# A row gradient streamed through three slots: the difference in three VectorE pieces with the halving on ScalarE, instead of one fused VectorE pass

## Chip, cores, metric

The kernel runs on one core of one Trainium2 chip. The metric is the device time of one execution in microseconds (us), as a median of several executions. The profile is one execution taken by the hardware profiler.

## The reference

```python
x = np.random.randn(8192, 8192).astype(np.float32)
return np.gradient(x, axis=1)
```

Inside a row the result is (x[j+1] - x[j-1]) / 2; the two ends take the plain difference of neighbours. The input is 268.44 MB and so is the output.

## The kernel before

A tile is R = 2 rows on each of 128 partitions, 64 KiB per partition; there are 32 tiles and three slots. A tile is loaded 64 elements into its slot, and the result is written from the slot's beginning, partly over the input. The store goes out from there; the next load into the slot waits until that store has landed. Loads are issued by SP (SyncE), stores by ACT (ScalarE), the last two tiles' stores by SP.

```python
    slots = [pool.tile([P, SH + W], f32, name=f"slot{k}", tag=f"slot{k}") for k in range(NB)]   # NB = 3
    ...
    def load(i):
        b = slots[i % NB]
        ins = nc.sync.dma_start(out=b[:, SH : SH + W], in_=x_sets[i])
        loads.append(chain(i, ins, *(stores[i - NB] if i >= NB else [])))
    ...
            ins = nc.gpsimd.tensor_sub(                      # the end differences, on Pool
                out=ends[:, i, :, :],
                in0=xin[:, :, 1 : m : m - 2],
                in1=xin[:, :, 0 : m - 1 : m - 2],
            )
            ...
                ins = nc.vector._custom_dve(                 # (in0 - in1) * 0.5 in one pass
                    dve_ops.TENSOR_TENSOR_REDUCE_SUB_MAX,
                    out=b[:, c0:c1],
                    in0=b[:, SH + c0 + 1 : SH + c1 + 1],
                    in1=b[:, SH + c0 - 1 : SH + c1 - 1],
                    s0=0.0,
                    s1=0.5,
                )
                ...
                ins = placer.tensor_copy(out=res[:, :, 0 : m : m - 1], in_=ends[:, i, r : r + nr, :])
                ...
                cuts = [c0, c0 + FIRST, c1] if i == 1 else [c0, c1]   # store 1 in two pieces
                for a0, a1 in zip(cuts, cuts[1:]):
                    ins = queue.dma_start(out=out_sets[i, :, a0:a1], in_=b[:, a0:a1])
```

The last tile is worked in two halves, so that its first half can be stored early.

## Time and profile before

| | |
|---|---|
| time, first comparison | 1248.27 us median of 4 runs (1247.95 to 1248.54) |
| the run that was profiled | 1252.67 us, 4 us more than any of these |
| DVE (VectorE) busy | 554.8 us, 44% |
| Pool (GpSimd) busy | 8.8 us, 1% |
| both DMA queues' packets | 99.3% of 16 engines' span |
| landing of a tile to its store's issue | 17.7 us (22.74 to 40.44 for the first tile) |

A slot is in one of three states: loading, computing, storing. So the page's last part, the issues of transfers with the median time from issue to landing, gives two of these three. These two lines of the kernel before are what the argument turns on (the last number is the time in us):

```profile
slot<-in_x_dram SPq DMA_DIRECT2D x32, 43.7
out_dram<-slot ACTq DMA_DIRECT2D x29, 55.0
```

An 8.39 MB tile alone at 434 GB/s, the rate of many of the page's slices, would take 19.3 us (an estimate from these two numbers). That a load takes 43.7 and a store 55.0 means that they share the engines (the two queues' packets take 52.9 and 46.4% of the same 16 engines' span) and queue behind one another.

### The profile page before, as it was taken

The numbers are of one execution on the slowest core, as the hardware profiler recorded it, in microseconds if no ns is written. First come the engines' busy times: TensorE is split into PE (matmuls) and PEld (weight loads), VectorE is DVE, ScalarE is ACT, GpSimd is POOL, SyncE is SP. The second block draws the span as 40 slices with busy tenths as digits, with TensorE's granted clock in tenths as the row PEclk, the third lists the DMA queues.
The fourth block names the chain that finished last, engine by engine and source line by source line (L and its number), as shares of the span: only waits on it lengthen the run. The fifth ranks groups of instructions, "written<-read, shape, count | busy, mean of one in ns | idle before, by whom it ended". The sixth has DMA issues, their size and how long they took to land.

```text
span 1250.2 us, 266 instructions
## 1 busy us (share of the span) xinstructions
DVE 554.8 (44%) x54; POOL 8.8 (1%) x48
## 2 busy tenths in 40 slices
DVE  2841455335553255523555335553345533455443
POOL 0000000000000000000000000000000000000000
DMA  9999999999999999999999999999999999999996
GB/s 403 436 438 433 434 434 436 428 436 421 428 434 434 436 430 434 434 436 436 436 436 436 434 436 434 428 432 426 434 434 434 436 434 436 436 436 436 436 436 289
DMA packets 9504, 536.88 MB, mean 429 GB/s; under 512 B 1056, under 2 KB 1056, under 8 KB 1184
## 3 DMA queue, kind: packets, MB, share of 16 engines
q1 hardware_dynamic: 5040, 285.21, 52.9%
q10 hardware_dynamic: 4464, 251.66, 46.4%
HBM read 268.44 MB, written 268.44 MB: 429 GB/s over the span
## 4 chain that ended last, share of the span: by engine, by line
another core or an unknown queue 83%; DMA 9%; issue 3%; DVE 3%; SPq 1%; POOL 0%; POOLq 0%
DMA slot<-in_x_dram 5%; DMA out_dram<-slot 3%; DVE slot L81 3%; SPq L60 1%; DVE slot L92 0%; POOL ends L70 0%; POOLq L131 0%
## 5 line engine op out<-in xcount | busy, mean ns | idle before, releaser
L81 DVE CUSTOM_DVE_ANT_0 slot<-slot 128x16382 f32<-128x16382 f32 (+1 forms) x33 | 551.3, 16706 | 673.0 <-POOL ends L70 673.0
L70 POOL TENSOR_TENSOR ends<-slot 128x4 f32<-128x4 f32 x32 | 6.3, 198 | 993.9 <-DMA slot<-in_x_dram 993.9
L92 DVE COPY slot<-ends 128x4 f32<-128x4 f32 (+1 forms) x21 | 3.6, 171 | 0.7
L92 POOL COPY slot<-ends 128x4 f32<-128x4 f32 x12 | 2.3, 190 | 207.9 <-DVE slot L81 207.9
L120 POOL MEMSET const-bfloat16-1.0<- 128x1 bf16 x1 | 0.1, 102 | 0.0
L120 POOL MEMSET const-uint8-127<- 128x1 uint8 x1 | 0.1, 102 | 0.0
L120 POOL MEMSET const-float32-0.0<- 128x1 f32 x1 | 0.1, 98 | 0.2 <-issue 0.2
L120 POOL MEMSET const-float32-1.0<- 128x1 f32 x1 | 0.1, 98 | 0.0
## 6 DMA issues: line engine op xcount, KB each, us to landing
out_dram<-slot SPq DMA_DIRECT2D x2, 4096.0 KB, 20.3
out_dram<-slot ACTq DMA_DIRECT2D x1, 7744.0 KB, 58.0
slot<-in_x_dram SPq DMA_DIRECT2D x32, 43.7
out_dram<-slot ACTq DMA_DIRECT2D x29, 55.0
out_dram<-slot ACTq DMA_DIRECT2D x1, 448.0 KB, 22.8
out_dram<-slot SPq DMA_DIRECT2D x1, 37.7
```

What stands on the lines that cost most here:

```text
L60: ins = nc.sync.dma_start(out=b[:, SH : SH + W], in_=x_sets[i])
L70: ins = nc.gpsimd.tensor_sub(out=ends[:, i, :, :], in0=xin[:, :, 1 : m : m - 2], in1=xin[:, :, 0 : m - 1 : m - 2],)
L81: ins = nc.vector._custom_dve(dve_ops.TENSOR_TENSOR_REDUCE_SUB_MAX, out=b[:, c0:c1], in0=b[:, SH + c0 + 1 : SH + c1 + 1], in1=b[:, SH + c0 ...
L92: ins = placer.tensor_copy(out=res[:, :, 0 : m : m - 1], in_=ends[:, i, r : r + nr, :])
L120: nc = _bacc.Bacc("TRN2", target_bir_lowering=False, num_devices=1)
```

## The change

Its intent is to do without the custom instruction and without Pool: plain subtracts on DVE in three pieces, each halved on ACT while DVE works on the next. The end copies move to ACT. The small first piece of store 1 goes. The last tile keeps the custom pass.

```diff
-            ins = nc.gpsimd.tensor_sub(
+            ins = nc.vector.tensor_sub(
                 out=ends[:, i, :, :],
...
+                if last:
+                    ins = nc.vector._custom_dve(   # as before
...
+                else:
+                    cuts = [c0, W // 3, 2 * W // 3, c1]
+                    for a0, a1 in zip(cuts, cuts[1:]):
+                        ins = nc.vector.tensor_sub(
+                            out=b[:, a0:a1],
+                            in0=b[:, SH + a0 + 1 : SH + a1 + 1],
+                            in1=b[:, SH + a0 - 1 : SH + a1 - 1],
+                        )
+                        diff = chain(i, ins, *at)
+                        ins = nc.scalar.mul(out=b[:, a0:a1], in_=b[:, a0:a1], mul=0.5)
+                        halved = chain(i, ins, diff)
...
-                placer = nc.gpsimd if i % 5 in (1, 3) and not last else nc.vector
-                ins = placer.tensor_copy(out=res[:, :, 0 : m : m - 1], in_=ends[:, i, r : r + nr, :])
+                ins = nc.scalar.copy(out=res[:, :, 0 : m : m - 1], in_=ends[:, i, r : r + nr, :])
...
-                cuts = [c0, c0 + FIRST, c1] if i == 1 else [c0, c1]
-                for a0, a1 in zip(cuts, cuts[1:]):
-                    ins = queue.dma_start(out=out_sets[i, :, a0:a1], in_=b[:, a0:a1])
-                    stores[i].append(chain(i, ins, placed))
+                ins = queue.dma_start(
+                    out=out_sets[i, :, r * m : (r + nr) * m], in_=b[:, r * m : (r + nr) * m]
+                )
+                stores[i].append(chain(i, ins, placed))
```

More of the change, by code (lines that the diff above doesn't have):

```diff
@@ L31 @@
     W = R * m
-    FIRST = 896
     nsets = n // (P * R)
@@ L79 @@
                 c0, c1 = r * m + 1, (r + nr) * m - 1
-                ins = nc.vector._custom_dve(
-                    dve_ops.TENSOR_TENSOR_REDUCE_SUB_MAX,
-                    out=b[:, c0:c1],
-                    in0=b[:, SH + c0 + 1 : SH + c1 + 1],
-                    in1=b[:, SH + c0 - 1 : SH + c1 - 1],
-                    s0=0.0,
-                    s1=0.5,
-                )
-                halved = chain(i, ins, *at)
+                if last:
+                    ins = nc.vector._custom_dve(
+                        dve_ops.TENSOR_TENSOR_REDUCE_SUB_MAX,
+                        out=b[:, c0:c1],
+                        in0=b[:, SH + c0 + 1 : SH + c1 + 1],
+                        in1=b[:, SH + c0 - 1 : SH + c1 - 1],
+                        s0=0.0,
+                        s1=0.5,
+                    )
+                    halved = chain(i, ins, *at)
+                else:
[9 more added lines that the diff above has]
+                        halved = chain(i, ins, diff)
@@ L90 @@
                 res = b[:, r * m : (r + nr) * m].rearrange("p (t m) -> p t m", m=m)
-                placer = nc.gpsimd if i % 5 in (1, 3) and not last else nc.vector
-                ins = placer.tensor_copy(out=res[:, :, 0 : m : m - 1], in_=ends[:, i, r : r + nr, :])
+                ins = nc.scalar.copy(out=res[:, :, 0 : m : m - 1], in_=ends[:, i, r : r + nr, :])
                 placed = chain(i, ins, halved)
                 queue = nc.scalar if i < nsets - 2 else nc.sync
-                c0, c1 = r * m, (r + nr) * m
@@ L99 @@
-                cuts = [c0, c0 + FIRST, c1] if i == 1 else [c0, c1]
-                for a0, a1 in zip(cuts, cuts[1:]):
-                    ins = queue.dma_start(out=out_sets[i, :, a0:a1], in_=b[:, a0:a1])
-                    stores[i].append(chain(i, ins, placed))
+                ins = queue.dma_start(
+                    out=out_sets[i, :, r * m : (r + nr) * m], in_=b[:, r * m : (r + nr) * m]
+                )
+                stores[i].append(chain(i, ins, placed))
                 at = [halved]
```

## The prediction

> **What bounds the kernel now.** I read the page's first three parts first, because they say at once whether an engine or the transfers carry the span.
>
> ```profile
> span 1250.2 us, 266 instructions
> DVE 554.8 (44%) x54; POOL 8.8 (1%) x48
> DMA  9999999999999999999999999999999999999996
> GB/s 403 436 438 433 434 434 436 428 436 421 428 434 434 436 430 434 434 436 436 436 436 436 434 436 434 428 432 426 434 434 434 436 434 436 436 436 436 436 436 289
> q1 hardware_dynamic: 5040, 285.21, 52.9%
> q10 hardware_dynamic: 4464, 251.66, 46.4%
> ```
>
> The busiest compute engine works 44% of the span; the DMA row is full in 39 of 40 slices and the two queues' packets together take 99.3% of sixteen engines' time. The bytes are fixed: 268.44 MB in, 268.44 MB out. The trace's packet records agree: nearly every 64 KiB packet takes 2.418 us, on either queue. There are 8,192 such rows' worth in all, 512 per DMA engine, so 512 x 2.418 = 1238.0 us that no order of instructions can remove. The first packet begins at 1.8 us. In the landing records of the very last store, most engines finish at 1240.5 to 1242.6 us and the slowest at 1249.3. So the span is the floor, a start of 2 us, and about 9 us by which one DMA engine is late.
>
> Next, is a transfer ever waiting for compute? The groups by shape give the durations, the waits of the sync engine's queue say what releases loads, and the timeline gives one period.
>
> ```profile
> L81 DVE CUSTOM_DVE_ANT_0 slot<-slot 128x16382 f32<-128x16382 f32 x31 | 533.9, 17224 | 654.4 <-POOL ends L70 654.4
> L81 DVE CUSTOM_DVE_ANT_0 slot<-slot 128x8190 f32<-128x8190 f32 x2 | 17.4, 8686 | 18.6 <-POOL ends L70 18.6
> L92 DVE COPY slot<-ends 128x4 f32<-128x4 f32 x19 | 3.3, 172 | 0.6
> L92 POOL COPY slot<-ends 128x4 f32<-128x4 f32 x12 | 2.3, 190 | 207.9 <-DVE slot L81 207.9
> ...
> SPq L60 <- DMA out_dram<-slot: 1156.3, 29, 79.5
> ```
>
> A load into a slot waits for the store out of it, 29 times for 1156.3 us: the queue of loads is held by transfers, not by arithmetic. The chain of waits that ended last shows the same at the tail:
>
> ```profile
> 1174.77 35.83 issue
> 1210.60 0.24 POOLq L131
> 1210.84 0.02 issue
> 1210.87 8.70 DVE slot L81
> 1219.57 0.02 issue
> 1219.59 0.17 DVE slot L92
> 1219.76 8.60 DVE slot L81
> ```
>
> The last load has landed by 1210.6; DVE then needs two passes of 8.7 us, and still 20 us of stores follow. By the landing records the store of the tile before lands on its slowest engine at 1229.9, so both halves of the last tile (issued at 1219.8 and 1228.6) are queued before that engine runs dry.
>
> **A period and its slack.** Loads are issued every 38.7 us (16 packets per engine at 2.418 us are 38.7, so the slowest engine is never idle). A slot goes round in three periods, 116.1 us: median 43.7 us from a load's issue to landing, 17.7 us of compute (the first tile: Pool starts at 22.74, the store goes out at 40.44), 55.0 us from store issue to landing; the sum is 116.4. For both queues to hold at least one transfer all the time, load and store together need two periods, 77.4 us. So compute could take about 38.7 us, twice what it takes, before even one queue ran empty; and a single queue can use all the engines alone: in the first 25 us, with loads alone, the rate is already 419 GB/s.
>
> [...] The custom pass shows just this: (17224 - 8686)/(16382 - 8190) = 1.042 ns per element and 151 ns fixed. [...]
>
> **The change part by part.**
>
> 1. *Difference on DVE.* Pieces of 5460, 5461 and 5461 elements. [...] 5461 x 1.042 + 151 = 5.84 us each, 17.53 us for three, 0.30 more than one pass, for two more fixed costs. The end differences move from Pool (198 ns) to DVE (about 170, as its copies of four elements). DVE in total: 31 x 17.70 + 17.4 + 0.2 = about 566 us, 45%.
>
> 2. *Halving on ACT.* [...]
>
> 3. *End copies on ACT*, after the halving: about 0.19 us, like the 170 to 190 ns of DVE and Pool.
>
> From landing to store issue: [...] 22.7 us, against 17.7: 5.0 us more per tile, 155 us over 31 tiles if all were exposed. By the slack above (about 21 us per slot) none is. What must give is time spent queueing: three periods still make 116.1, so load plus store to landing fall from 98.7 to about 93.5, and since a store is queued behind the one before it, I expect the median store to land about 5 us sooner after issue (near 50 us) with the load's near 43.7. The store's wait shortens, its end doesn't move.
>
> 4. *Head.* The first store moves from 40.4 to about 45.4. The three loads issued at the start are 3 x 19.4 = 58 us of work at full rate, so the engines have work; the load that shared with store 0 now runs alone for those 5 us. Cost 0.
>
> 5. *Tail.* The last tile keeps the custom pass, so 1210.6 to the two stores gains only ACT's hand-off, some 0.1 us each. Store 30 goes out near 1197 instead of 1192.3. The last load lands on its earliest engines at 1201.5, on its slowest at 1210.6, and store 30 is behind it in the same queue: still on time, with 4 us to spare on the earliest engines and 13 on the slowest. Cost 0 to 1.
>
> 6. *Store 1 in one piece.* The small first piece (448 KB, 3.5 KB packets) disappears. Same bytes; eight fewer small packets an engine. What it can move is the phase between the queues, and with it which engine gets late. I put this at a few us of either sign.
>
> Sum: 1248.1 + 0 (steady) + 0 (head) + 0.5 (tail) + about 1 (a tuned phase is disturbed, more likely to lose than to gain) = 1249.5 us.
>
> **The rivals.**
>
> *The latency is exposed.* If slots went strictly one after the other, 31 x 5.0 = 155 us: about 1403. It would need a queue that waits for compute. Against it: the DMA row of nines, and twice the compute time fits. Half-exposed, at head and tail only: 10 us, 1258. Against it: points 4 and 5.
>
> *ACT becomes the bound, or its work delays the stores it issues.* ACT issues stores in its own order, after the copy. [...] If halving were twice as slow [...], the time from landing to store would be about [...] 35 us: nearly at the 38.7 us limit, yet still about 1250. [...]
>
> *The passes contend with the transfers for the buffer memory.* ACT would add a read and a write of every element. For the present passes the windows of the trace show no steady sign:
>
> ```profile
> 515.20:532.40 17.20, 17.18 (x1) 0.00 (x0) 1.00 1.04 450
> 532.40:554.30 21.90, 0.05 (x1) 0.19 (x1) 1.00 1.02 443
> 554.60:571.80 17.20, 17.19 (x1) 0.00 (x0) 1.00 0.98 427
> 571.80:593.30 21.50, 0.17 (x1) 0.00 (x0) 1.00 1.02 439
> ```
>
> With DVE busy 450 and 427 GB/s, with it idle 443 and 439. Bins of whole packets explain such scatter. If ACT slowed transfers by 1%, 1261.
>
> *The lateness of one DMA engine changes.* It is 9 us now, built up by load packets of 2.5 to 3.6 us instead of 2.418, nearly all in the first 660 us. With another phase it could vanish (1241) or double (1258). This is the rival I take most seriously, and it sets the range.
>
> **Range and chances.** Executions of one kernel differ by 0.6 us, so the width is from the phase and a little contention: 1245 to 1256 for 8 in 10. Two per cent is 25 us: 1223 is below the floor of 1238, so faster is all but impossible (0.01). Slower than 1273 needs exposed latency or contention: 0.03.
>
> **What would show each step.** Right: the DMA row stays at 9 in 39 slices and about 434 GB/s; DVE near 45% with 5.8 us pieces; [...] first store near 45.4; store to landing near 50 us at the median; sync's waits for stores still over 1100 us; two or more transfers pending throughout. Wrong: DMA slices below 9 in the middle, or a store-bound wait replaced by one for ACT (latency exposed); packets longer than 2.418 us while ACT runs (contention); full DMA on most engines but a last landing far behind the others (engine lateness).

The 22.7 us from landing to store was a sum with a term for ACT's last piece, which no trace stood behind, and the second rival's 35 us the same. So 22.7 and 35 us stand as estimates. That a plain subtract runs at the custom pass's rate was assumed too. Measured after the prediction: 4755 ns for an ACT piece, 5848 ns for a DVE piece, with the custom pass as with the plain subtract. The forecast's zeros for the middle and the head rest on the 22.7. Its floor of 1238 us rests on the packets: of the 64 KiB ones none is shorter than 2.418 us in the profiles of the two kernels, and 98% (before) and 96% (changed) took under 2.43.

## The result

The changed kernel takes 1249.45 us, median of 4 runs (1248.41 to 1249.82), against 1248.27 us. The ratio is 1.0008, 95% interval 0.9991 to 1.0026: the same. Ratios in this document are the mean time of one kernel's fast runs over that of the other's of the same rounds, so not quite the ratio of the quoted medians.

The head of the changed kernel's page, its two DMA queues and its issues:

```profile
span 1247.6 us, 419 instructions
DVE 566.6 (45%) x127; ACT 450.0 (36%) x127; POOL 0.2 (0%) x4
DMA  9999999999999999999999999999999999999998
q1 hardware_dynamic: 5040, 285.21, 53.1%
q10 hardware_dynamic: 4320, 251.66, 46.6%
...
slot<-in_x_dram SPq DMA_DIRECT2D x32, 43.7
out_dram<-slot ACTq DMA_DIRECT2D x30, 49.6
```

ACT works for 450 us that did not exist before, and the DMA row is as full as it was. The load's median is still 43.7 us; the store's has fallen from 55.0 to 49.6. The work itself, by groups of one shape (busy us and mean ns after the bar):

```profile
L93 DVE TENSOR_TENSOR slot<-slot 128x5461 f32<-128x5461 f32 x62 | 362.6, 5848 | 2.1
L99 ACT ACTIVATE slot<-slot 128x5461 f32<-128x5461 f32 x62 | 294.8, 4755 | 69.9 <-DVE slot L93 69.9
...
L102 ACT COPY slot<-ends 128x4 f32<-128x4 f32 x31 | 6.1, 198 | 1.0
L69 DVE TENSOR_TENSOR ends<-slot 128x4 f32<-128x4 f32 x32 | 5.3, 166 | 655.9 <-DMA slot<-in_x_dram 655.9
```

An ACT piece is shorter than a DVE piece, so ACT waits for each (69.9 us over 62 pieces) and only the third one trails. The timeline of tile 30 shows the order (start, duration, what):

```profile
1171.93 0.17 DVE L69 TENSOR_TENSOR ends<-slot 128x4 f32<-128x4 f32 x1 [20.82 <-DMA slot<-in_x_dram]
1172.13 17.61 DVE L93 TENSOR_TENSOR slot<-slot 128x5460 f32<-128x5460 f32 x3
1178.01 4.75 ACT L99 ACTIVATE slot<-slot 128x5460 f32<-128x5460 f32 x1 [21.89 <-DVE slot L93]
1183.89 4.75 ACT L99 ACTIVATE slot<-slot 128x5461 f32<-128x5461 f32 x1 [1.13 <-DVE slot L93]
1189.77 4.75 ACT L99 ACTIVATE slot<-slot 128x5461 f32<-128x5461 f32 x1 [1.13 <-DVE slot L93]
1194.56 0.20 ACT L102 COPY slot<-ends 128x4 f32<-128x4 f32 x1
1194.78 31.53 SPq L105 DMA_DIRECT2D out_dram<-slot  x3
```

From 1171.93 to 1194.78 are 22.85 us from landing to store; before they were 17.7. The loads still wait for stores and for nothing else:

```profile
SPq L59 <- DMA out_dram<-slot: 1153.8, 29, 79.6
```

Before, 29 such waits made 1156.3 us. A slot's round is 43.7 + 17.7 + 55.0 = 116.4 us before and 43.7 + 22.9 + 49.6 = 116.2 after: the 5.2 us that the tile computes longer came off the time until its store has landed.

The landing records say where. Each transfer lands sixteen times (1056 landings for the 66 transfers of the kernel before), once on each DMA engine, and the page counts to the last. These are medians in us from issue to landing (the last two rows are experiments below, the last of them a slow run):

| run | landing to store | load: first, last engine | store: first, eighth, last engine |
|---|---|---|---|
| before | 17.7 | 40.3, 43.7 | 42.3, 42.6, 55.0 |
| changed | 22.9 | 40.5, 43.7 | 42.7, 43.7, 49.6 |
| after_uncut | 31.6 | 39.5, 43.8 | 39.5, 39.8, 41.6 |
| after_pieces_two_passes | 34.7 | 39.4, 42.5 | 39.1, 40.5, 43.3 |

So on the first eight engines to land, a store took no less time than before. What shrank is the lag of the last engine behind the first, from 12.7 to 7.0 us; the next load into the slot waits for that last one. The three experiments that change one part agree: 42.1 and 49.0 us to the first and the last landing in after_split_store, 43.5 and 55.0 in before_whole_store, 41.1 and 55.2 in after_no_act_halving.

### The profile page after: what moved, and what is told of

Read it like the earlier page. It is cut to its first block, busy times and chain, and to the rows that moved or that the text cites. A ratio compares the mean times of both kernels' runs of the same rounds, so it can differ in the third digit from the quotient of the medians.

```text
span 1247.6 us, 419 instructions
## 1 busy us (share of the span) xinstructions
DVE 566.6 (45%) x127; ACT 450.0 (36%) x127; POOL 0.2 (0%) x4
## 4 chain that ended last, share of the span: by engine, by line
DMA 68%; DVE 14%; another core or an unknown queue 12%; ACT 4%; issue 0%; SPq 0%
DMA out_dram<-slot 35%; DMA slot<-in_x_dram 33%; DVE slot L93 13%; ACT slot L99 3%; DVE slot L81 1%; ACT slot L102 0%; DVE ends L69 0%; SPq L59 0%
## 5 line engine op out<-in xcount | busy, mean ns | idle before, releaser
L99 ACT ACTIVATE slot<-slot 128x5461 f32<-128x5461 f32 (+1 forms) x93 | 442.2, 4755 | 743.4 <-DVE slot L93 743.4
L93 DVE TENSOR_TENSOR slot<-slot 128x5461 f32<-128x5461 f32 (+1 forms) x93 | 543.9, 5848 | 3.2
L69 DVE TENSOR_TENSOR ends<-slot 128x4 f32<-128x4 f32 x32 | 5.3, 166 | 655.9 <-DMA slot<-in_x_dram 655.9
L102 ACT COPY slot<-ends 128x4 f32<-128x4 f32 (+1 forms) x33 | 6.5, 197 | 31.8 <-DVE slot L81 30.8
L81 DVE CUSTOM_DVE_ANT_0 slot<-slot 128x8190 f32<-128x8190 f32 x2 | 17.4, 8691 | 0.1
L99 ACT ACT_TABLE_LOAD x1 | 1.3, 1283 | 0.7 <-PEq L126 0.7
## 6 DMA issues: line engine op xcount, KB each, us to landing
slot<-in_x_dram SPq DMA_DIRECT2D x32, 43.7
out_dram<-slot ACTq DMA_DIRECT2D x30, 49.6
```

The costliest lines, as they stand in the source:

```text
L69: ins = nc.vector.tensor_sub(out=ends[:, i, :, :], in0=xin[:, :, 1 : m : m - 2], in1=xin[:, :, 0 : m - 1 : m - 2],)
L81: ins = nc.vector._custom_dve(dve_ops.TENSOR_TENSOR_REDUCE_SUB_MAX, out=b[:, c0:c1], in0=b[:, SH + c0 + 1 : SH + c1 + 1], in1=b[:, SH + c0 ...
L93: ins = nc.vector.tensor_sub(out=b[:, a0:a1], in0=b[:, SH + a0 + 1 : SH + a1 + 1], in1=b[:, SH + a0 - 1 : SH + a1 - 1],)
L99: ins = nc.scalar.mul(out=b[:, a0:a1], in_=b[:, a0:a1], mul=0.5)
L102: ins = nc.scalar.copy(out=res[:, :, 0 : m : m - 1], in_=ends[:, i, r : r + nr, :])
```

## The experiments

The theory: the DMA engines are the bound, the added 5 us per tile lie in the transfers' waiting time, and ACT's arithmetic does not slow the transfers. The rivals: part of the time shows; ACT's extra traffic slows transfers; or one of the small parts (the split store, Pool) mattered and cancelled something else.

Three figures of each profile's packet records help to read the runs. *Excess*: the packets' time beyond 2.418 us per 64 KiB, summed and divided by the 16 DMA engines. *Idle*: the time to the last packet's end less the packets' time, again per engine. *Drained*: how many transfers were issued onto a queue whose former transfer had landed on all 16 engines (or did so within 1 us). Every kernel moves 1238.0 us of nominal packets per engine. Packet records can overlap a little (two idle times below, 0.0 and 0.4 us, are less than the 1.76 us before the first packet of the kernel before), so an idle time near zero is rough. The rows of after_pieces_two_passes and before_two_slots are profiles of runs that count as slow (1309.94 and 1341.74 us).

| run | slots x tile | landing to store, us | median us | excess, us | idle, us | drained |
|---|---|---|---|---|---|---|
| before | 3 x 64 KiB | 17.7 | 1248.3 | 3.2 | 7.8 | 1 of 66 |
| changed | 3 x 64 | 22.9 | 1249.5 | 4.5 | 4.0 | 1 of 65 |
| after_split_store | 3 x 64 | 22.9 | 1251.5 | 3.1 | 4.5 | 1 of 66 |
| before_whole_store | 3 x 64 | 17.7 | 1256.9 | 2.9 | 8.8 | 1 of 65 |
| after_no_act_halving | 3 x 64 | 18.1 | 1254.3 | 3.4 | 13.3 | 1 of 65 |
| after_uncut | 3 x 64 | 31.6 | 1257.2 | 11.4 | 2.4 | 1 of 65 |
| after_pieces_two_passes | 3 x 64 | 34.7 | 1308.4 | 48.5 | 20.2 | 19 of 65 |
| after_two_act_passes | 3 x 64 | 45.5 | 1354.6 | 58.0 | 57.1 | 46 of 65 |
| after_62us | 3 x 64 | 62.7 | 1393.4 | 55.0 | 96.9 | 59 of 65 |
| before_two_slots | 2 x 64 | 17.7 | 1329.2 | 50.6 | 49.3 | 49 of 66 |
| after_two_slots | 2 x 64 | 22.9 | 1357.2 | 52.8 | 77.0 | 56 of 65 |
| before_half_tiles | 6 x 32 | 9.2 | 1246.9 | 5.7 | 0.0 | 0 of 128 |
| half_tiles_two_passes | 6 x 32 | 23.3 | 1247.3 | 5.5 | 0.4 | 1 of 128 |
| after_half_tiles_uncut | 6 x 32 | 16.2 | 1263.3 | 11.2 | 6.9 | 0 of 128 |

The experiments were noisier than the first comparison: the kernel before itself gave 1246.8 to 1270.6 us (11 runs, median 1252.1) in the first batch, 1246.6 to 1260.1 in the second, 1247.9 to 1258.7 in the third. So medians of different batches must not be compared to a few us; the ratios below are each against the kernel before on the same chip. A run over 1.5% above its kernel's fastest counts as slow and is left out of the ratios.

### Undoing one part, or doing one alone

**after_split_store**: the changed kernel with store 1 in two pieces again.

```diff
-                ins = queue.dma_start(
-                    out=out_sets[i, :, r * m : (r + nr) * m], in_=b[:, r * m : (r + nr) * m]
-                )
-                stores[i].append(chain(i, ins, placed))
+                d0, d1 = r * m, (r + nr) * m
+                for a0, a1 in ([(d0, d0 + 896), (d0 + 896, d1)] if i == 1 else [(d0, d1)]):
+                    ins = queue.dma_start(out=out_sets[i, :, a0:a1], in_=b[:, a0:a1])
+                    stores[i].append(chain(i, ins, placed))
```

> The changed kernel with one part undone: store 1 again in two pieces (448 KB first). Theory (the bytes bind; the split only shifts the phase between the two queues): 1247 to 1251 us, within 0.3% of the changed kernel, ACT and DVE busy times unchanged. Rival (the split was what kept the late DMA engine's lag down): nearer to the kernel before, about 1248.2, and the spread of the last store's sixteen landings different from the changed kernel's 5 us.

Measured: 1251.51 us (1247.87 to 1257.07), ratio 0.9997 (0.9959 to 1.0035), the same. The median is just above the stated range, on a chip where before stood at 1252.05. The landings of the very last store spread over 5.4 us, near the changed kernel's 5.2 (before: 8.8; one profile each). In these profiles the split did not set this spread.

**before_whole_store**: the kernel before with `cuts = [c0, c1]` for every store.

> The kernel before with one part of the change done alone: all stores in one piece, custom pass and Pool work kept. Theory: 1247 to 1251 us, ratio to before within 0.2%. Rival (the split matters): slower than before by over 0.3%, that is over 1252.

Measured: 1256.86 us (1247.84 to 1268.4), ratio 1.0028 (0.998 to 1.0077). The median lies above the range and beyond the rival's 1252, but the interval holds 1, so a cost of the whole store of up to 0.8% is neither shown nor excluded. The last landings spread over 8.9 us, as before's 8.8.

**after_no_act_halving**: the three pieces stay, but each is the custom pass that halves as it subtracts; ACT only places the ends.

```diff
-                        ins = nc.vector.tensor_sub(
+                        ins = nc.vector._custom_dve(
+                            dve_ops.TENSOR_TENSOR_REDUCE_SUB_MAX,
                             out=b[:, a0:a1],
...
+                            s0=0.0,
+                            s1=0.5,
                         )
-                        diff = chain(i, ins, *at)
-                        ins = nc.scalar.mul(out=b[:, a0:a1], in_=b[:, a0:a1], mul=0.5)
-                        halved = chain(i, ins, diff)
+                        halved = chain(i, ins, *at)
```

> The changed kernel with the halving folded back into the custom DVE pass, still three pieces a tile, end copies still on ACT, so ACT does no arithmetic on the bulk. From landing to store about 17.9 us instead of 22.9. Theory (5 us per tile are hidden, ACT does not disturb the transfers): 1248 to 1250.5 us, the same as the changed kernel within 0.2%, but the median store takes about 55 us from issue to landing again instead of 49.6. Rival (ACT's extra reads and writes of the buffer slow transfers, or part of the latency shows): faster than the changed kernel by 0.3% or more, 1245 or less.

Measured: 1254.34 us (1245.81 to 1258.1), ratio 1.0005 (0.9963 to 1.0048); above the range, and so was before on this chip. Taking 442 us of ACT arithmetic away made nothing faster that could be seen; the interval leaves room for 0.4%. As the intervals of these three runs all lie within 0.8% of the kernel before, a larger cost of one of these parts that another cancels is excluded. Pool's work was not undone alone. The groups by shape and the issues of this run:

```profile
L93 DVE CUSTOM_DVE_ANT_0 slot<-slot 128x5461 f32<-128x5461 f32 x62 | 362.6, 5848 | 2.1
...
out_dram<-slot ACTq DMA_DIRECT2D x30, 55.2
```

The custom pass takes 5848 ns, to the nanosecond what the plain subtract takes: halving was free in it. And the store takes 55.2 us again. The round is 44.1 + 18.1 + 55.2 = 117.4: the time from landing to store and the store's time to its last landing trade nearly one for one.

### More latency on the same three slots

**after_uncut**: one subtract, then one ACT pass over the whole tile (`cuts = [c0, c1]`).

> The changed kernel with the tile in one piece: one 17.2 us subtract, then one ACT pass of about 13.9 us, so about 31.6 us from landing to store, 9 us more than with pieces. Theory (compute is hidden as long as it takes under 38.7 us a tile): 1248 to 1252 us; the median store lands about 41 us after its issue instead of 49.6. Rival (latency shows in part): more than the changed kernel by several us, up to 31 x 8.7 = 270 us if all shows. The pieces would be worth nothing if the theory holds.

Measured: 1257.23 us (1253.5 to 1262.16), ratio 1.0045 (1.0004 to 1.0085). ACT's pass took 13.86 us a tile and the subtract 17.22. The store's median fell to 41.6 us as expected, and yet the runs are 0.45% slower than before, some 5.6 us:

```profile
slot<-in_x_dram SPq DMA_DIRECT2D x32, 43.8
out_dram<-slot ACTq DMA_DIRECT2D x30, 41.6
```

That is 2% of the 270 us which full exposure would cost, but it may not be nothing: the interval just leaves out 1. The table says in what form it comes: excess 11.4 us instead of 3.2, that is slower packets, with no more idle time. So the pieces may be worth a little.

The landing records fit a reason. 53 of 63 transfers were issued when the one before them on their queue had landed on some engines already, or did so within 1 us (1 in the changed kernel), and 220 of the 221 store packets that ran 3% or more over 2.418 us start within 4.5 us of a store's issue. But this count alone does not set the loss: it is 31 in after_no_act_halving, whose excess is 3.4 us.

**after_two_act_passes**: uncut, with two ACT passes, so that the result stays right.

```diff
-                        ins = nc.scalar.mul(out=b[:, a0:a1], in_=b[:, a0:a1], mul=0.5)
-                        halved = chain(i, ins, diff)
+                        for by in (2.0, 0.25):
+                            ins = nc.scalar.mul(out=b[:, a0:a1], in_=b[:, a0:a1], mul=by)
+                            halved = chain(i, ins, diff)
```

> Uncut tile and two ACT passes over it (times 2, times a quarter; the result is still right): about 17.4 + 2 x 13.9 + 0.3 = 45 us from landing to store, past the 38.7 us; ACT busy 28 us per period, so no engine binds. Theory (work of the DMA engines never stops while a transfer is queued): past 38.7 us two slots are in compute at once, and at the turn from store to load of the third no transfer is queued for some 1.5 to 2.3 us (0.3 to the landing, 1.1 from issue to the first packet, up to 0.8 of slow first packet): 31 x that on 1249 = 1295 to 1320 us. Rival A (exposure in proportion to the excess): 45 - 38.7 = 6.3 us x 31 = 195: about 1445. Rival B (never exposed before two slots' compute exceeds the period): 1250 to 1255.

Measured: 1354.57 us (1348.38 to 1355.98), ratio 1.0787 (1.0713 to 1.086). All three figures miss: it is less than in proportion and more than one dry turn a tile. The parts of the 1.5 to 2.3 us compare with the first load of the kernel before: its last landing came 0.35 us after its last packet's end, its first packet began 1.02 us after its issue, and each engine's first packet ran 0.08 to 0.99 us over 2.418. The rows of the page for DMA:

```profile
DMA  9799999999999999999999999998999999999999
GB/s 410 333 393 437 434 407 368 370 362 418 372 374 434 434 403 391 408 408 372 403 432 401 401 376 405 403 418 356 403 403 403 403 377 397 352 408 379 377 434 403
```

The reader should note how little the digits show: 9 means 90% or more, and the loss is in GB/s. By the records, 46 of 65 transfers went onto a drained queue, loads and stores alike, where I had counted one turn per tile. The loss beyond the nominal packets is half slow packets (58.0 us) and half idle (57.1). Beyond before's 11.0 us that is 104 us, or 2.3 us for each of the 46. If the whole loss is put on these, the cost of one turn was guessed about right (1.5 to 2.3 us); their number was not.

**after_62us**: the same, with the subtract done twice.

```diff
-                        ins = nc.vector.tensor_sub(
+                        for _ in range(2):
+                            ins = nc.vector.tensor_sub(
...
```

> As the last, and the subtract done twice over on DVE (same values): about 62 us from landing to store, DVE 34.6 and ACT 27.9 us per period of 38.7, so no engine binds yet. Theory: a turn from store to load without any other transfer, once a tile, as at 45 us: 1295 to 1330 us, and the DMA row below full throughout. Rival A (proportional): (62 - 38.7) x 31 = 722 more: about 1970. Rival B: 1250 to 1260.

Measured: 1393.42 us (1391.17 to 1395.71), ratio 1.1113. The result is wrong, against what I wrote: the first subtract overwrites input that the second reads, as the result lies over the input. The two subtracts took 34.48 us and the two ACT passes 27.74 in the tiles whose timeline was read; in after_two_act_passes, whose result is right, one subtract took 17.22 and the two ACT passes 27.74. So the wrong values show in no duration, and the time stands as a measurement of latency only. 59 transfers met a drained queue, and the loss beyond before's is 141 us, 2.4 us each on the same terms. No run came near the proportional 1970 us.

**after_pieces_two_passes**: the changed kernel with those two passes over each of the three pieces: the case that the prediction named.

> The changed kernel, three pieces, with two ACT passes over each (the case that the prediction named: 35 us from landing to store). A round of three periods leaves about 81 us for load and store, against 77.4 for two queues that never run empty. Theory, as mended after the runs at 45 and 62 us (each transfer issued onto an empty queue costs about 2.1 us, one half of it slow packets, one half idle): few such issues, under 15, so 1252 to 1275 us. The prediction said about 1250. Rival A (all time beyond 22.7 us shows in proportion): 31 x 12 = 370 us more. Rival C (more ACT arithmetic itself slows the transfers, as 1354 us with two passes could also be read): near 1354, as there are the same two passes.

Measured: 1308.38 us: three runs of 1306.8 to 1310.9 and one of 1286.08. The three count as slow only because the one is 1.5% quicker, so no ratio is given; every run is over 2% above the slowest run of before in its batch (1258.73). So at 34.7 us from landing to store, which leaves more than two periods for load and store, the time rises already, and neither the prediction's "still about 1250" nor my mended 1252 to 1275 held. Rivals A (370 us more) and C (near 1354) missed too. The issues of its profile, a slow run:

```profile
slot<-in_x_dram SPq DMA_DIRECT2D x32, 42.5
out_dram<-slot ACTq DMA_DIRECT2D x30, 43.3
```

Both are over the 38.7 us of a period, yet 19 transfers met a drained queue. The loss beyond before's is 58 us there, 3.0 us for each of the 19, so drained queues are hardly all of it.

### Is it ACT's work, or the latency?

**half_tiles_two_passes**: the very kernel that took 1354.6 us, with tiles of one row per partition and six slots. Bytes in flight and arithmetic per byte are the same; only the time from landing to store, and the size of one step and of its packets, halve.

```diff
-    R = 2
-    NB = 3
+    R = 1
+    NB = 6
```

> The uncut tile with two ACT passes that took 1354 us, now with tiles of half the size and six slots: the same bytes in flight, the same arithmetic per byte, about 23 us from landing to store against a period of 19.4 and a round of 116. Theory (what costs is an empty queue, and here 93 us are left for load and store where 38.7 keep both queues filled): 1246 to 1257 us, at most three issues onto an empty queue. Rival C (two ACT passes slow the transfers): over 1330 again.

Measured: 1247.28 us (1247.1 to 1247.33), ratio 0.9962 (0.9929 to 0.9995).

```profile
DVE 566.5 (45%) x128; ACT 899.2 (72%) x191; POOL 0.2 (0%) x4
...
GB/s 404 421 438 438 422 437 438 432 427 438 437 426 434 437 437 423 437 437 431 429 438 437 426 432 438 437 424 436 438 429 429 438 438 424 435 438 435 425 437 391
...
slot<-in_x_dram SPq DMA_DIRECT2D x64, 4096.0 KB, 43.6
out_dram<-slot ACTq DMA_DIRECT2D x62, 4096.0 KB, 49.3
```

ACT is busy for 899 us, twice as long as in the changed kernel, and the transfers run at full rate. This shows that the 1354.6 us did not come from ACT's traffic by itself but from latency against three coarse slots. The round is six periods: 43.6 + 23.3 + 49.3 = 116.2 us.

**before_half_tiles**: the kernel before with R = 1, NB = 6 and whole stores.

> The kernel before with tiles of half the size, six slots and all stores whole. Theory: the two queues were never empty before, so there is nothing to win in the middle: 1244 to 1253 us, within 0.4% of before. Rival (packets of 32 KB cost more): over 1260.

Measured: 1246.94 us (1246.82 to 1247.56), ratio 0.996 (0.9933 to 0.9987), with 71.3 + 9.2 + 35.6 = 116.1 us a round. It is 0.4% better than the kernel before, and steady: its runs lie within 0.8 us on a chip where before's lie within 11 (those of half_tiles_two_passes within 0.3). The landings of its last store spread over 1.5 us: the engines finish nearly together.

**after_half_tiles_uncut**: the changed kernel uncut, with R = 1, NB = 6.

> The changed kernel uncut, with tiles of half the size and six slots: about 16.5 us from landing to store. Theory: the 0.45% that the uncut tile cost with three slots goes away, 1244 to 1253 us, the same as before within 0.3%, and the DMA engines' excess over 2.418 us per 64 KiB falls from 11 us to 3 to 5. Rival (the cut itself, ACT working beside DVE, was what helped): 1253 to 1260 again.

Measured: 1263.28 us (1254.97 to 1276.53), ratio 1.0067 (1.0022 to 1.0113). This misses. Two ACT passes took 1247.3 us, one takes longer. No queue drained, but the excess is 11.2 us, with 611 packets that ran over their 1.213 us by more than 0.05 us (47 and 42 in the two other half-tile runs), and the landings of its last six stores spread over 10 to 25 us. So slow packets come also where neither latency nor an empty queue explains them. That takes weight from after_uncut too: its excess of 11.4 us may have the same unknown cause, and not its thin margin. What makes a given order of the two queues fall into or out of this, no run here settles.

### Two slots

**before_two_slots** and **after_two_slots**: NB = 2 in either kernel.

> The kernel before with two slots instead of three. From landing to store 17.7 us, and a slot's round is two periods. Theory: while one slot computes only the other transfers, and its turn from store to load falls in the middle of that time, so 1.5 to 2.3 us per tile are lost: 1295 to 1320 us. Rival (buffer count sets how much of the compute shows): 31 x some 10 us more, over 1500.

> The changed kernel with two slots. Theory: the loss is the turn alone, not the compute time, as long as that is under 38.7 us: the same as the kernel before with two slots within 0.5%, 1295 to 1320 us. Rival (with scarce slots the 5 us more show): 31 x 2.5 to 5 us more than the kernel before with two slots, 80 to 155 us.

Measured: before 1329.23 us over all runs (1299.49, 1316.73, and two called slow, 1341.74 and 1346.15), ratio of the fast ones 1.0433 (1.0315 to 1.055); changed 1357.15 us (1355.04 to 1371.19), ratio 1.0847 (1.0767 to 1.0927). The changed kernel is slower than before here: the theory's "the same within 0.5%" fails, the rival's 80 to 155 us too. 49 transfers in the one and 56 in the other met a drained queue. The size of the difference is uncertain, since before with two slots varies by 47 us; its direction is not, as every run of the one is above every run of the other. So with three slots the change is free and with two it costs some 4%. That it is the 5 us of latency, and no other part of the change, that costs there is argued: with two slots no part was undone alone.

## Why the prediction was right, point by point

- **The bound.** Right. The DMA row stayed full; ACT gained 450 us of work and the time moved by 1.2 us, within noise.
- **DVE.** 17.53 us for three pieces was worked out, 17.61 measured (the timeline), 566.6 us busy against "about 566". The fixed part was read as 151 ns; the two lengths leave 150 (17224 - 1.0422 x 16382). Nothing hangs on it.
- **ACT.** 4.755 us a piece and 450.0 us busy, 36%, were measured. The profile also has an ACT_TABLE_LOAD of 1283 ns, at 0.73 us into the span and out of the way: the first tile's load landed at 22.6.
- **Landing to store.** 22.7 put down, with an estimate in it for ACT's piece; 22.85 measured.
- **Where it is hidden.** The median store was to land near 50 us after issue and the load to stay near 43.7; they are 49.6 and 43.7. after_no_act_halving gives the 55 us back. This is the step that carries the prediction, and as a sum it is shown by measurement. Its reason, that the store is queued behind the one before it, is only half right: to the first engine's landing the store took 42.3 us before and 42.7 after. What gave way was the last engine's lag.
- **Head.** The first store was to move to about 45.4; it went out at 45.50.
- **Tail.** Store 30 went out at 1194.78, not 1197, because the whole schedule of that profile is 2.6 us earlier; the last load landed at 1208.1, after it, as needed.
- **Store 1 and the phase.** "A few us of either sign" is as much as can be said after the runs too. The 1.2 us between the medians is not resolved.
- **The sum.** 1248.1 + 0.5 + 1 is 1249.6, not 1249.5. That 1249.45 was measured is luck at this closeness: the 1.5 us were guesses for the tail and the phase, and in the experiments one kernel's runs differ by some 10 us.
- **What was wrong in it.** The second rival's aside: at about 35 us from landing to store the time would be "still about 1250". Measured: 1286 to 1311. The step that failed is the slack: it was taken as sharp at 38.7 us, and counted on the median of the last engine's landing. A large cost is there at 34.7 us, and a first, small one (0.45%) perhaps at 31.6. A load is issued only when the last engine's part of a store has landed (0.02 to 0.09 us after it in the kernel before), and until then the engines that landed first get nothing new for that slot: for 12.7 us at the store's median. In the kernel before the first engine had 40.3 + 42.3 = 82.6 us of load and store, 5 us over two periods and not 21; the other 16 us were waiting for the last engine. In these profiles the added latency came out of that lag first, without a visible cost. In after_uncut 4.3 us of lag were left at the load and 2.1 at the store, which puts the limit at 38.7 - 6.4 = 32.3 us: an estimate made after the runs, which no run of its own tested. Also "executions differ by 0.6 us" held in the first comparison alone.
- **The lateness of one engine.** The rival taken most seriously. In the profiles the spread of the last landings goes with the latency (8.8 and 8.9 us at 17.7, 8.9 at 18.1, 5.2 and 5.4 at 22.9, 2.3 at 31.6), one profile each, but no gain in the median followed. The table by engines shows the same over the whole run: the lag shrinks as the latency grows. Why one engine falls behind at all stays open.

## What to carry to other kernels

With a full DMA row, add up a slot's round (load to landing, landing to store, store to landing): here added latency came off the time to the last landing first (5.2 us, of a store's 55.0) and cost nothing that could be seen while both queues still held work with a margin. Count that margin on the engine that lands first, not on the last, and do not spend it down to the computed limit: here the loss was clear 4 us below it, and perhaps began 7 us below. Smaller tiles in more slots can buy margin: two ACT passes were free with six half-size slots and cost 8% with three. It is no sure cure, as after_half_tiles_uncut was 0.7% slower than the kernel before.

## The DMA queues in these traces

- If the whole loss of a run is put on the transfers issued onto drained queues, it is 2.3 and 2.4 us each in the three-slot runs with 46 and 59 of them, 3.0 in the one with 19, and 1.8 and 2.1 with two slots; part of it is packets of up to 4.7 us instead of 2.418.
- In the kernel before the first load's first packet began 1.0 us after its issue on idle engines, and the first store's 6.2 us after issue (40.44 to 46.64) while loads held the engines.
- The 16 engines drift apart under two busy queues: up to 16 us between first and last landing of one store in the kernel before, 9 us of it left at the end, and up to 27 us in after_no_act_halving.
